# Attention merge moved to VectorE in half rows, a copy moved to ScalarE, and two small TensorE products moved to other PSUM banks

## The chip, the core and the metric

The kernel runs on one core of a Trainium2 chip. The core has five engines that work side by side: TensorE (PE in the profile; its weight loads are listed as PEld), VectorE (DVE), ScalarE (ACT), GpSimd (POOL) and SyncE (SP, which here issues the transfers). The metric is the device time of one execution in microseconds; lower is better. A "bank" is one of the eight parts of the accumulation memory (PSUM) that TensorE writes to and that VectorE and ScalarE read.

## What is computed

One layer of a hybrid decoder for a prompt of 1024 tokens and a sample group of 8 sequences of 8 new tokens (1088 columns in all), float32 throughout. One input projection gives queries, keys and values of three attention groups, gates, and the inputs of a state-space scan. The part that matters here is the merge of the three attention groups, for each pair of heads:

```python
def _combine_groups(outs, lses):
    w = jax.nn.softmax(jnp.stack(lses, 0), axis=0)
    o = jnp.einsum('gblh,gblhd->blhd', w.astype(outs[0].dtype), jnp.stack(outs, 0))
    return o.reshape(o.shape[0], o.shape[1], ATT_WIDTH)
```

that is, att = w0*o0 + w1*o1 + w2*o2, then times SiLU of a gate path. The three groups look back with dilations 1, 4 and 16. Sample attention runs over a cache of past keys and values and is added in the same layout. After that come the scan, two branch projections, an output projection and a final norm.

## The kernel before, in words

Channels lie on the 128 partitions and tokens along the row. The work has four phases: a front (norm and modulation), attention, the scan (SSD) and the output projections. In attention and scan TensorE's main work is the input projection, cut into jobs of 128 output channels (`run`, L260). A job has three chunks of 368, 368 and 352 columns, and each chunk eight steps of three matmuls (`mm3`, L195: high part, low part and cross term), written as "pj" in the profile. Each job loads its weights and splits them into whi (ScalarE, L191) and wlo (VectorE, L192).

**The order on TensorE is the order of the code.** Between the steps of a projection, `Order` lets a generator, the side work, put its own matmuls in. A generator yields a number of nanoseconds (or an event and a number); it goes on when the planned time has passed that. Nothing is waited for on the chip by this: it only places the instructions. The order on the other engines is set by a scheduler when the program is built; it isn't written out in the code. It may run an instruction of later code ahead of one of earlier code.

**Attention.** For each of four head pairs hp and three groups g, `attention` (L548) turns the values (vt, vts; copied out by VectorE, L573 and L576), then `prompt_group` (L590) makes scores (s), which VectorE reduces with the mask (L617) and ScalarE exponentiates (L620), turns the result (pt; copied out by ScalarE L641 and VectorE L639) and multiplies it by the values (o, copied out by ScalarE L661). After group 2 come `sample_scores` and `sample_values` (L766): seven and three small transposes of the sample's probabilities (spt), products with the cached values accumulated in the bank so, a copy of it to the tile so (L798), a pause of the planner (L799), two transposes of the copy (soT, L803) and four VectorE instructions that gate the result into the first group's output (L807). The transposes of the next head pair's values follow soT at once in TensorE's order.

**The merge** is `combine` (L717). Its inputs are the group outputs oT[0..2], in each group's own token order (`group_view`, L477, reads them in natural order: steps of 256 elements for dilation 4 and of 64 for dilation 16), and the weights, which `weights` (L681) wrote to memory and six transfers bring back spread over the partitions (L722, tiles wb). It is traced with `issue_after(last)`: those of its instructions that run on VectorE come after the last L807; its GpSimd instructions aren't held by that. The result goes to memory (L733) and is read in the last phase.

**Banks.** In the attention phase the eight banks are three for projections, two of kind A (scores), two of kind B (transposes) and one of kind C (vts, o, so). In the scan phase they are three, two A and three B. A tile of a kind takes the bank that was taken longest ago and waits until its last reader is done. In the scan phase the side work (L919) turns the tokens of B (to_tokens, kind B, L924), 15,000 planned ns after projection C makes the products CB (kind A, two tiles, masked by VectorE in L938) and one small product for the sample (L940 to L942); after these TensorE goes back to projection steps. Meanwhile VectorE runs the convolution of the next channel tile, three instructions that each use the one before (L869).

Of the kernel before, what the change touches and what calls it, by code (L numbers as in the profile page):

```python
# [11 lines left out]
AF = mybir.ActivationFunctionType  # L12
OP = mybir.AluOpType
# [4 lines left out]
T = 1024  # L18
# [5 lines left out]
DIL = (1, 4, 16)  # L24
# [86 lines left out]
def trunk(ctx: ExitStack, tc: tile.TileContext, I, O):  # L111
    nc = tc.nc
    V, S, G, PE, SP = nc.vector, nc.scalar, nc.gpsimd, nc.tensor, nc.sync
# [15 lines left out]
    def bank(kind):  # L129
        return lambda name: banks[kind].tile([128, 512], F32, tag=kind, name=name)  # L130

    bankA, bankB, bankC, bankPJ = bank("a"), bank("b"), bank("c"), bank("p")
# [15 lines left out]
    def P(name):  # L148
        a, n = PACK[name]
        return pack[:, a:a + n]  # L150
# [11 lines left out]
    def sums(ps, sq, first=True, last=True):  # L162

        for j in range(4):
            PE.matmul(ps[j * 32:j * 32 + 32, :QT], onesc[:, :32], sq[:, j * QT:(j + 1) * QT], start=first, stop=last,
                      tile_position=(0, j * 32))
# [39 lines left out]
    def mm(out, w, x, ns, **kw):  # L206
        PE.matmul(out, w, x, **kw)  # L207
        order.spend(ns)

    def turn(out, x, eye):  # L210
        PE.transpose(out, x, eye)  # L211
        order.spend(110)
# [79 lines left out]
    with pool("ph0", 2) as p0:  # L292
# [51 lines left out]
        with tc.high_priority():  # L344
            ps = bankA("ms")
# [7 lines left out]
            for j in range(4):  # L353
                ps = (bankPJ if j < 3 else bankC)("rb")
# [122 lines left out]
    def group_view(ap, g):  # L477

        return ap.rearrange("p (r i) -> p i r", r=DIL[g])
# [3 lines left out]
    with ExitStack() as actx:  # L483
# [233 lines left out]
        def combine(hp, oT, ga):  # L717
            at = oT[0]
            for g in range(3):
                wb = ap_.tile([128, T], F32, tag="kv", name="wb", bufs=5)  # L720
                for h in range(2):
                    SP.dma_start(out=wb[h * 64:h * 64 + 64], in_=bass.AP(tensor=wt_d.tensor, offset=wt_d[hp, g, h].offset,  # L722
                                                                         ap=[[0, 64], [1, T]]))
                src = group_view(oT[g][:, :T], g)
                if g == 0:
                    V.tensor_mul(at[:, :T], at[:, :T], wb)
                else:
                    d = DIL[g]
                    w3 = wb.rearrange("p (i r) -> p i r", r=d)
                    G.tensor_tensor(w3, src, w3, op=OP.mult)  # L730
                    V.tensor_add(at[:, :T], at[:, :T], wb)
            V.scalar_tensor_tensor(at[:, :T], at[:, :T], 0.5, ga[:, :T], op0=OP.mult, op1=OP.mult)
            SP.dma_start(out=att_d[hp], in_=at)  # L733

        def sample_scores(hp, ks):
# [30 lines left out]
        def sample_values(hp, sm, vs, at):  # L766
            yield 9000.0,
            pT = a1.tile([128, 7, 128], F32, tag="spT", name="spT")
            pN = a1.tile([TS, 3, 128], F32, tag="spN", name="spN")
            for i, n in ((0, 4), (4, 3)):  # L770
                pt = bankB("spt").rearrange("p (x n) -> p x n", n=128)
                for x in range(n):
                    turn(pt[:, x, :], sm[:, (i + x) * 128:(i + x + 1) * 128], ident)
                S.activation(pT[:, i:i + n, :], pt[:, :n, :], AF.Copy)
            pt = bankB("spt").rearrange("p (x n) -> p x n", n=128)
            for g in range(3):
                turn(pt[:TS, g, :], sm[:, 896 + g * TS:896 + (g + 1) * TS], ident)
            S.activation(pN, pt[:TS, :3, :], AF.Copy)

            yield 3000.0,  # L780
            po = bankC("so")
            for g in range(3):
                PE.matmul(po[:, :256].rearrange("p (e n) -> p e n", e=2), pN[:, g, :],
                          vs[:, g:g + 1, :].to_broadcast([TS, 2, 128]), start=g == 0, stop=False)
            vts = []
            for x in range(7):
                vt = ap_.tile([128, NB, 128], F32, tag="kv", name="vt", bufs=5)
                SP.dma_start(out=vt, in_=I["vc"][hp, x])
                vts.append(vt)
            for x, vt in enumerate(vts):  # L790
                if x in (0, 5):
                    yield (500.0 if x == 0 else 8000.0),
                for e in range(2):
                    for j in range(4):
                        mm(po[j * 32:j * 32 + 32, e * 128:(e + 1) * 128], pT[:, x, j * 32:j * 32 + 32],
                           vt[:, 2 * j + e, :], 70.0, start=False, stop=x == 6 and e == 1)
            so = a1.tile([128, 7, 128], F32, tag="spT", name="so")
            V.tensor_copy(so[:, 0:2, :].rearrange("p e n -> p (e n)"), po[:, :256])  # L798
            yield 1500.0,  # L799
            ga = tiles[hp, "ga"]  # L800
            po = bankB("soT")
            for e in range(2):
                turn(po[:, e * 128:(e + 1) * 128], so[:, e, :], ident)  # L803
            for e in range(2):
                for h in range(2):
                    hs = slice(h * 64, h * 64 + 64)
                    last = V.scalar_tensor_tensor(at[hs, T:].rearrange("p (b s) -> p b s", b=NB)[:, e::2, :],  # L807
                                           po[hs, e * 128:(e + 1) * 128].rearrange("p (b x) -> p b x", b=NB)[:, e::2, h * 8:h * 8 + 8],
                                           0.5, ga[hs, T:].rearrange("p (b s) -> p b s", b=NB)[:, e::2, :],
                                           op0=OP.mult, op1=OP.mult)  # L810
            return last
# [9 lines left out]
    with ExitStack() as bctx:  # L821
# [3 lines left out]
        cb = b1.tile([128, 24], F32, name="cb")  # L825
# [93 lines left out]
        def side():  # L919
            for gr in range(4):  # L920
                yield ("B", gr), 15000.0
                B = BT, BS = tiles.pop(("B", gr))
                Bk = b1.tile([128, 9, 128], F32, tag="Bk", name="Bk")
                to_tokens(B, lambda c0, n, ps: S.activation(Bk[:, c0:c0 + n, :], ps, AF.Copy))  # L924

                Bs = b1.tile([128, 128], F32R, tag="Bs", name="Bs")
                S.activation(Bs, Bk[:, 8, :], AF.Copy)
                V.tensor_sub(Bs[TS:], Bk[TS:, 8, :], Bs[TS:].bitcast(F32))
                yield ("C", gr), 15000.0
                CT, CS = tiles.pop(("C", gr))  # L930
                CB = b1.tile([128, TT], F32, tag="CB", name="CB")
                G.memset(CB[TS:, T:], 0.0)
                for q in range(2):
                    ps = bankA("cb").rearrange("p (c n) -> p c n", c=4)
                    for c in range(4):
                        sl = slice((4 * q + c) * 128, (4 * q + c + 1) * 128)
                        mm(ps[:, c, :], BT[:, sl], CT[:, sl], 224.0, start=True, stop=True)
                    V.tensor_tensor(CB[:, q * 512:(q + 1) * 512].rearrange("p (c n) -> p c n", c=4), ps,  # L938
                                    P("causal")[:, None, :].to_broadcast([128, 4, 128]), op=OP.mult)
                ps = bankA("cb")  # L940
                mm(ps[:TS, :TS], BS[:, :TS], CS[:, :TS], 224.0, start=True, stop=True)
                V.tensor_tensor(CB[:TS, T:], ps[:TS, :TS], P("causal_s")[:TS], op=OP.mult)  # L942
                order.passed.add(("B", gr))
                sq = b1.tile([128, TT], F32, tag="sq", name="sq")
                for xt in range(4 * gr, 4 * gr + 4):
                    yield from x_tile(gr, xt, Bk, Bs, CB, CT, CS, sq)
                    order.passed.add(("x", xt))

                yield 4000.0,
                ps = bankB("ms")  # L950
                sums(ps, sq)
                ms = bp.tile([128, 3, QT], F32, tag="ms", name="ms", bufs=1)
                rms(ms, ps, 512)
                for j in range(4):
                    SP.dma_start(out=rs_d[gr:gr + 1, j * QT:(j + 1) * QT], in_=ms[j * 32:j * 32 + 1, 1, :])
# [147 lines left out]
    with pool("yr", 2) as yr, pool("yw", 2) as yw:  # L1103
# [31 lines left out]
        for gr in range(5):  # L1135
            if gr:
                if gr < 4:
                    ys = load_ys(gr)
                else:
                    ys = []  # L1140
                    for i in range(4):
                        x = yr.tile([128, TT], F32, tag="yx", name="ax")
                        SP.dma_start(out=x, in_=att_d[i])
                        ys.append(split(x))
            for m in range(8):
# [14 lines left out]
                for c0, cn in CHUNKS:  # L1160
                    sl = slice(c0, c0 + cn)
                    ps = bankPJ("pj")
# [23 lines left out]
    for t in range(9):  # L1186
        n = min(128, TT - t * 128)
        x = f2.tile([128, D], F32, tag="fx", name="fx")
# [6 lines left out]
        for i in range(m):  # L1195
            ps = bankA("fo")[:n, :w]
            cs = slice(i * w, (i + 1) * w)
# [14 lines left out]
        for i in range(2):  # L1212
            cs = slice(i * 512, (i + 1) * 512)
# [152 lines left out]
```

## Time and profile before

| what | us |
|---|---|
| median of 3 runs (1919.27 to 1925.73) | 1921.6 |
| the profiled execution, its own time | 1926.49 |
| its span, first to last instruction | 1924.7 |
| TensorE busy | 1872.7 (97%) |
| VectorE busy | 1020.1 (53%) |
| ScalarE busy | 664.1 (35%) |
| GpSimd busy | 393.2 (20%) |
| mean granted clock of TensorE | 0.992 |

The span is one execution; an engine's busy time is the part of it in which it had an instruction running. A timeline row gives the start, the length, the engine, the line of the code, the operation, output and inputs with partitions x elements, and in brackets how long the engine had been idle before and what ended that idle time. "x2" means that adjacent instructions were merged into one row. The granted clock is a share of TensorE's full 2.4 GHz.

### The profile page before, as it was taken

The page shows a single profiled execution, that of the slowest core. Times are in us where ns is not written, and L with a number is a line of the kernel's source. Part 1 is how long each engine was busy: PE and PEld are TensorE (multiplying, and loading weights), DVE is VectorE, ACT ScalarE, POOL GpSimd, SP SyncE. Part 2 cuts the span into 40 slices and gives each one's busy share as a digit, 9 for nine tenths or more (in the row PEclk, how much of TensorE's full clock was granted, in tenths as well). Part 3 has the DMA queues.
Part 4 walks back from the last instruction along what each step waited for, and adds up shares of the span by engine and source line. Part 5 has one row for each costly group of instructions (what it writes and reads, how often), then busy time and mean ns, then how long its engine had stood idle before and what let it go on. Part 6 is the DMA issues. An engine that isn't in the chain of part 4 may idle for free.

```text
span 1924.7 us, 32199 instructions
## 1 busy us (share of the span) xinstructions
PE 1872.7 (97%) x13057; PEld 1748.8 (91%) x13057; DVE 1020.1 (53%) x1918; ACT 664.1 (35%) x1271; POOL 393.2 (20%) x584
## 2 busy tenths in 40 slices
PE   6999999999999999999999999999999999999998
PEld 4999989989998998999989998999898989999987
DVE  4633243334334323467675776577657665566654
ACT  4434234314432432424352434243433332131222
POOL 3100010010001001124513542444244300000400
PEclk8999999999999999999999999999999999999999
DMA  8422562273246227435444444444233364364322
GB/s 329 138 79 92 158 200 83 90 220 114 96 159 194 84 89 240 143 121 171 148 142 137 148 154 132 137 138 138 82 102 105 126 223 137 121 196 153 119 88 77
DMA packets 108949, 269.56 MB, mean 140 GB/s; under 512 B 41581, under 2 KB 50593, under 8 KB 105537
## 3 DMA queue, kind: packets, MB, share of 16 engines
q1 hardware_dynamic: 108800, 267.51, 42.2%
q8 instruction: 102, 1.67, 0.4%
q14 instruction: 47, 0.38, 0.1%
HBM read 224.93 MB, written 80.26 MB: 159 GB/s over the span
## 4 chain that ended last, share of the span: by engine, by line
PE 58%; DVE 4%; ACT 3%; DMA 2%; issue 1%; POOL 0%; DVEq 0%; ACTq 0%; POOLq 0%
PE pj L198 15%; PE pj L199 15%; PE pj L200 15%; PE fo L1203 2%; PE fo L1201 2%; PE fo L1202 2%; PE yd L207 2%; PE yo L207 2%; DMA csb<-cs_d 2%; PE stt L207 1%; PE tt L211 1%; DVE xc L869 1%; PE sts L207 1%; DMA yx<-u_d 1%; PE o L207 0%
## 5 line engine op out<-in xcount | busy, mean ns | idle before, releaser
L198 PE MATMUL pj<-h_hi,whi 128*128 128x368 f32 x2256 | 753.9, 334 | 0.0
L199 PE MATMUL pj<-h_hi,wlo 128*128 128x368 f32 x2256 | 739.1, 328 | 0.0
L200 PE MATMUL pj<-h_lo,whi 128*128 128x368 f32 x2256 | 739.0, 328 | 0.0
L198 PEld LDWEIGHTS pj<-h_hi,whi 128*128 128x128 f32 x2256 | 424.8, 188 | 25.3 <-issue 22.8
L199 PEld LDWEIGHTS pj<-h_hi,wlo 128*128 128x128 f32 x2256 | 425.0, 188 | 0.7
L200 PEld LDWEIGHTS pj<-h_lo,whi 128*128 128x128 f32 x2256 | 424.6, 188 | 0.0
L192 DVE TENSOR_TENSOR wlo<-wraw,whi 128x1024 fp32r<-128x1024 f32 (+1 forms) x136 | 158.1, 1162 | 253.6 <-ACT whi L191 251.7
L191 ACT ACTIVATE whi<-wraw 128x1024 fp32r<-128x1024 f32 (+1 forms) x136 | 126.5, 930 | 351.6 <-PE pj L200 334.3
L198 PE MATMUL pj<-yhi,whi 128*128 128x368 f32 (+1 forms) x480 | 158.3, 330 | 2.5 <-DVE acc L1165 2.5
L199 PE MATMUL pj<-yhi,wlo 128*128 128x368 f32 (+1 forms) x480 | 157.8, 329 | 0.1
L200 PE MATMUL pj<-ylo,whi 128*128 128x368 f32 (+1 forms) x480 | 157.5, 328 | 0.0
L620 ACT ACTIVATE pr<-pr,st 128x128 f32<-128x128 f32 (+1 forms) x192 | 83.9, 438 | 89.3 <-DVE st L617 89.2
L198 PEld LDWEIGHTS pj<-yhi,whi 128*128 128x128 f32 x480 | 90.6, 189 | 5.4 <-DVE acc L1165 3.0
L199 PEld LDWEIGHTS pj<-yhi,wlo 128*128 128x128 f32 x480 | 90.7, 189 | 1.8 <-DVE wlo L192 0.4
L200 PEld LDWEIGHTS pj<-ylo,whi 128*128 128x128 f32 x480 | 90.5, 189 | 0.0
L869 DVE SCALAR_TENSOR_TENSOR xc<-raw,cw,xc 128x1112 f32<-128x1112 f32 x60 | 82.5, 1376 | 10.6 <-ACT xc L867 9.8
L639 DVE COPY pT<-pt 128x512 f32<-128x512 f32 x40 | 27.6, 689 | 102.3 <-ACT pT L641 40.4
L1170 POOL TENSOR_TENSOR acc<-acc,ta 128x368 f32<-128x368 f32 (+1 forms) x24 | 24.2, 1010 | 253.1 <-DVE ta L1169 253.1
L559 POOL COPY ks<-k 128x64 f32<-128x64 f32 x12 | 6.7, 558 | 301.5 <-DVE k L500 301.5
L997 POOL TENSOR_TENSOR xde<-xdt,tok 128x256 f32<-128x256 f32 x64 | 43.1, 702 | 120.3 <-DVE xdt L990 120.3
L500 DVE COPY k<-pj 128x368 f32<-128x368 f32 (+2 forms) x44 | 24.1, 581 | 81.3 <-PE pj L200 79.8
L964 DVE TENSOR_TENSOR csb<-tok,csb 128x2048 f32<-128x2048 f32 x16 | 39.4, 2464 | 46.8 <-DMA csb<-cs_d 43.1
(269 smaller groups left out, 2613.5 us busy)
## 6 DMA issues: line engine op xcount, KB each, us to landing
wraw<-in_w_in SPq DMA_DIRECT2D x96, 512.0 KB
csb<-cs_d SPq DMA_DIRECT2D x16, 1088.0 KB
kt<-in_kc SPq DMA_DIRECT2D x32, 448.0 KB
out_kc<-in_kc SPq DMA_DIRECT2D x32, 448.0 KB
out_vc<-in_vc SPq DMA_DIRECT2D x28, 512.0 KB
vt<-in_vc SPq DMA_DIRECT2D x28, 512.0 KB
sg_d<-sg SPq DMA_DIRECT2D x16, 544.0 KB
ecs<-cs_d SPq DMA_DIRECT2D x32, 272.0 KB
```

Of the source, the lines that this page charges most:

```text
L191: S.activation(hi, raw, AF.Copy)
L192: V.tensor_sub(lo, raw, hi.bitcast(F32))
L198: PE.matmul(ps, whi[:, k, :], xhi[k], start=first and k == 0, stop=False)
L199: PE.matmul(ps, wlo[:, k, :], xhi[k], start=False, stop=False)
L200: PE.matmul(ps, whi[:, k, :], xlo[k], start=False, stop=last and k == n - 1)
L207: PE.matmul(out, w, x, **kw)
L620: S.activation(pr[:, h, c0:c0 + m], pr[:, h, c0:c0 + m], AF.Exp, scale=-1.0, bias=st[:, 0, h, u:u + 1], accum_out=st[:, 1, h, u:u + 1])
L869: V.scalar_tensor_tensor(c, raw[:, t:t + CONV], cw[:, j, t:t + 1], c, op0=OP.mult, op1=OP.add)
L964: V.tensor_tensor(csb[:, :, :T].rearrange("p h (c l) -> p h c l", l=CH), tok[:, :8, 32 + h0:34 + h0].rearrange("p c h -> p h c")[:, :, :, ...
L997: G.tensor_tensor(xde[:, c:c + 2].rearrange("p c (h d) -> p c h d", h=2), xdt[:, c:c + 2, :].rearrange("p c (h d) -> p c h d", h=2), tok[: ...
L1201: PE.matmul(ps, hi, whi[:, k, cs], start=k == 0, stop=False)
L1202: PE.matmul(ps, lo, whi[:, k, cs], start=False, stop=False)
```

## The change

In the merge, the two multiplications by weights that GpSimd did for each head pair go to VectorE, and all the merge's arithmetic is cut into two halves of 512 columns. The copy of the sample outputs goes from VectorE to ScalarE, and the planner's pause before soT goes from 1500 to 2500 ns. The third batch of sample transposes takes a bank of kind C in place of B; the scan's small product takes one of kind B in place of A.

```diff
@@ combine, from L724 @@
                 src = group_view(oT[g][:, :T], g)
-                if g == 0:
-                    V.tensor_mul(at[:, :T], at[:, :T], wb)
-                else:
-                    d = DIL[g]
-                    w3 = wb.rearrange("p (i r) -> p i r", r=d)
-                    G.tensor_tensor(w3, src, w3, op=OP.mult)
-                    V.tensor_add(at[:, :T], at[:, :T], wb)
-            V.scalar_tensor_tensor(at[:, :T], at[:, :T], 0.5, ga[:, :T], op0=OP.mult, op1=OP.mult)
+                d = DIL[g]
+                w3 = wb.rearrange("p (i r) -> p i r", r=d)
+                for x in range(2):
+                    cs = slice(x * 512, x * 512 + 512)
+                    i = slice(x * 512 // d, (x + 1) * 512 // d)
+                    if g == 0:
+                        V.tensor_mul(at[:, cs], at[:, cs], wb[:, cs])
+                    else:
+                        V.tensor_tensor(w3[:, i], src[:, i], w3[:, i], op=OP.mult)
+                        V.tensor_add(at[:, cs], at[:, cs], wb[:, cs])
+                    if g == 2:
+                        V.scalar_tensor_tensor(at[:, cs], at[:, cs], 0.5, ga[:, cs], op0=OP.mult, op1=OP.mult)
             SP.dma_start(out=att_d[hp], in_=at)
@@ sample_values, L775 @@
-            pt = bankB("spt").rearrange("p (x n) -> p x n", n=128)
+            pt = bankC("spt").rearrange("p (x n) -> p x n", n=128)
@@ sample_values, L798 @@
-            V.tensor_copy(so[:, 0:2, :].rearrange("p e n -> p (e n)"), po[:, :256])
-            yield 1500.0,
+            S.activation(so[:, 0:2, :].rearrange("p e n -> p (e n)"), po[:, :256], AF.Copy)
+            yield 2500.0,
@@ side, L940 @@
-                ps = bankA("cb")
+                ps = bankB("cb")
                 mm(ps[:TS, :TS], BS[:, :TS], CS[:, :TS], 224.0, start=True, stop=True)
```

## Rows read from the trace of the kernel before

**Rows 1.** The page, part 1: busy time, share of the span and instructions of each engine

```profile
PE 1872.7 (97%) x13057; PEld 1748.8 (91%) x13057; DVE 1020.1 (53%) x1918; ACT 664.1 (35%) x1271; POOL 393.2 (20%) x584
```

**Rows 2.** Waits of PE: engine, line, releaser: us in total, times, longest

```profile
PE soT L211 <- DVE so L798: 6.0, 3, 2.5
PE cb L207 <- DVE CB L938: 4.7, 4, 1.7
PE yo L207 <- DVE sta L1023: 3.5, 3, 1.2
PE spt L211 <- ACT spT L774: 3.2, 4, 0.8
PE pt L211 <- ACT pr L620: 0.8, 1, 0.8
```

**Rows 3.** Timeline of PE, first merge: start us, us, instruction [idle before <-releaser]

```profile
263.87 0.44 PE L211 MATMUL soT<-pack,so 128*128 128x128 f32 x2 [1.81 <-DVE so L798]
265.28 0.63 PE L211 MATMUL vt<-pack,vT 128*128 128x128 f32 x4 [0.54 <-DVE oT L807]
272.46 0.82 PE L211 MATMUL pt<-pack,pr 128*128 128x128 f32 x6
```

**Rows 4.** Timeline of DVE, first merge

```profile
260.02 3.46 DVE L192 TENSOR_TENSOR wlo<-wraw,whi 128x1024 fp32r<-128x1024 f32 x1 [0.40 <-ACT whi L191]
263.40 0.41 DVE L798 COPY so<-so 128x256 f32<-128x256 f32 x1
264.34 0.80 DVE L807 SCALAR_TENSOR_TENSOR oT<-soT,ga 64x32 f32<-64x32 f32 x4 [0.53 <-PE soT L211]
265.17 2.12 DVE L726 TENSOR_TENSOR oT<-oT,wb 128x1024 f32<-128x1024 f32 x1
267.31 1.29 DVE L573 COPY v<-vt 128x512 f32<-128x512 f32 x2
268.71 1.21 DVE L731 TENSOR_TENSOR oT<-oT,wb 128x1024 f32<-128x1024 f32 x1
269.85 0.27 DVE L617 CUSTOM_DVE_ANT_0 pr<-s,msk 128x128 f32<-128x128 f32 x1
```

**Rows 5.** Timeline of POOL, first merge

```profile
259.48 6.72 POOL L730 TENSOR_TENSOR wb<-oT,wb 128x1024 f32<-128x1024 f32 x2 [27.60 <-DMA wb<-wt_d]
```

**Rows 6.** Timeline of DVE and PE, third merge

```profile
594.08 1.23 DVE L192 TENSOR_TENSOR wlo<-wraw,whi 128x1024 fp32r<-128x1024 f32 x1 [0.40 <-ACT whi L191]
596.37 0.80 DVE L807 SCALAR_TENSOR_TENSOR oT<-soT,ga 64x32 f32<-64x32 f32 x4 [0.73 <-PE soT L211]
603.18 0.28 DVE L617 CUSTOM_DVE_ANT_0 pr<-s,msk 128x128 f32<-128x128 f32 x1
605.52 0.93 PE L211 MATMUL pt<-pack,pr 128*128 128x128 f32 x5 [0.77 <-ACT pr L620]
```

**Rows 7.** Windows, behind the fourth merge: us, busy of PE, PEld, DVE, ACT, POOL, PEclk, DMA

```profile
765.00:769.50 4.50, 4.41 (x18) 4.41 (x19) 3.81 (x7) 0.43 (x1) 2.45 (x1) 0.62 0.63 233
```

**Rows 8.** Timeline of ACT, first merge

```profile
270.17 0.40 ACT L620 ACTIVATE pr<-pr,st 128x128 f32<-128x128 f32 x1 [10.18 <-DVE st L617]
272.88 0.38 ACT L641 ACTIVATE pT<-pt 128x256 f32<-128x256 f32 x1 [0.25 <-PE pt L211]
```

**Rows 9.** Timeline of DVE: key copies of a group with dilation 1, then 4

```profile
207.60 0.54 DVE L500 COPY k<-pj 128x368 f32<-128x368 f32 x1 [0.83 <-PE pj L200]
248.58 0.84 DVE L500 COPY k<-pj 128x368 f32<-128x368 f32 x1 [5.52 <-PE pj L200]
```

**Rows 10.** Timeline of DVE in the SSD phase, first small product

```profile
816.52 1.38 DVE L869 SCALAR_TENSOR_TENSOR xc<-raw,cw,xc 128x1112 f32<-128x1112 f32 x1 [0.63 <-ACT xc L867]
817.93 1.29 DVE L938 TENSOR_TENSOR CB<-cb,pack 128x512 f32<-128x512 f32 x2
819.14 1.37 DVE L869 SCALAR_TENSOR_TENSOR xc<-raw,cw,xc 128x1112 f32<-128x1112 f32 x1
820.42 0.21 DVE L942 TENSOR_TENSOR CB<-cb,pack 64x64 f32<-64x64 f32 x1
```

## The prediction

> **What bounds the kernel now.** I read the page's busy shares first: TensorE works 1872.7 us of a span of 1924.7 us, VectorE 53% of it, ScalarE 35%, GpSimd 20% [rows 1]. No other engine is near the span, so the time can fall only by the 52 us in which TensorE does nothing, or by a higher clock. The second view is the list of TensorE's waits [rows 2], and here the reader should look for the products that the diff touches. Three are there: the turn of the sample outputs (soT) waits 6.0 us behind their copy on VectorE, the small product of the scan phase (cb) 4.7 us behind the evacuation of the bank that it takes over, and the third sample transpose (spt) 3.2 us in the same way. Together that is 13.9 us.
>
> The third view is the timeline of one merge, engine by engine, to see why the copy is late. TensorE stands 1.81 us before soT [rows 3]. The copy L798 needs 0.41 us, but it starts at 263.40, behind a wlo subtraction of 3.46 us [rows 4]. That subtraction runs beside the two multiplications of GpSimd, 259.48 to 266.20 [rows 5]. Before the third merge the same subtraction starts ahead of GpSimd's and takes 1.23 us [rows 6]; there soT doesn't wait, which is why rows 2 count three waits for four merges. So GpSimd's work delays VectorE by some 2.2 us, and TensorE pays.
>
> The wait has a tail. Behind the fourth, the longest with 2.5 us, the granted clock is 0.62 over 4.5 us [rows 7], a mix of the two levels, 1.2 and 2.4 GHz: (1 - 0.62) x 4.5 = 1.7 us more.
>
> **The change part by part.**
> *Small product from bank kind A to B.* In the scan phase A has two buffers and both hold the two products just made; B has three, last used by the turns of B's tokens, which the planner puts 15 us earlier. The four waits go: -4.7. Behind the product TensorE has projection steps, which need nothing from VectorE, so nothing takes their place at once.
>
> *Third transpose from B to C.* C's one buffer is free since the last attention output was copied. The four waits go: -3.2. The next user of C, the accumulation of the sample outputs, now stands behind the copy of this transpose, but it reads that copy's result anyway, and the planner puts 3.0 us between.
>
> *Copy of the sample outputs on ScalarE, and 1.0 us more before soT.* ScalarE copied 128x256 from a bank in 0.38 us and had been idle for 10.18 us until 270.17 in the first merge [rows 8]. The cover is that idle stretch; without it TensorE would wait for what stands ahead of the copy on ScalarE, less the extra 1.0 us. The extra 1.0 us is two projection steps put ahead of soT instead of behind it, no added work. The three waits go: -6.0, and with them the slow clock: -1.7.
>
> *Merge on VectorE.* Gone are eight GpSimd multiplications and what they cost VectorE. A merge had four whole-row VectorE instructions; the second kind, L731, takes 1.21 us undisturbed, while L726 took 2.12 beside GpSimd [rows 4]. It will have twelve half-row ones. A 128x512 piece takes 1.29 / 2 = 0.65 us in a row as the two v copies did [rows 4]. That holds for the eight pieces that read and write in order. The other four read the group's output in steps of 256 or 64 elements, and the trace has no such read. Lower bound: 0.65, as if the step were free. Upper bound: GpSimd's own pace for it, 6.72 / 4 = 1.68 us a half. The nearest row is VectorE's own write in the same steps, 0.84 us against 0.54 for 368 in order [rows 9]; 0.65 x 0.84 / 0.54 = 1.0 us, and I take that. A rule of the Trainium skill speaks against the change here: SBUF — State Buffer, section Door 1, says that accesses that keep crossing into a new 16-byte line pay a penalty, which such a read always does. It gives no price; by it the 1.0 stands, and if only writes paid, the price would be 0.65 and my sum 4.2 us better. The merge is then 8 x 0.65 + 4 x 1.0 = 9.2 us of VectorE.
>
> That length costs nothing by itself; what matters is what queues behind it. After soT, TensorE turns the next group's values and makes its scores; VectorE must copy those (L573) and reduce the scores (L617), ScalarE the exponentials, before TensorE comes to pt. In the third merge L617 began 603.18 - 597.17 = 6.0 us after L807 ended and pt waited 0.77 [rows 6]; in the first it was 4.7 [rows 4] and pt didn't wait [rows 3]. So pt waits for whatever goes beyond 5.2 us. Which instructions of the merge go ahead of L617? The order is fixed when the program is built. In the scan phase a chain of three L869, each needing the one before, takes turns with products that became ready meanwhile, though their code stands later [rows 10]. So I expect the same here: the six pieces that need no other piece (two halves of group 0's product, four of the others') go first, 2 x 0.65 + 4 x 1.0 = 5.3 us, then the copies of v, 1.3, then L617 among the additions: 6.6 us or so, a wait of 1.4 at each of the first three merges, 4.2 in all, in place of the 0.8 of today. The bounds: 0 if the copies and L617 go first; if the whole merge goes ahead, 9.2 + 1.3 - 5.2 = 5.3 each. The fourth merge has no attention behind it, so its delay is covered by projections.
>
> *Sum.* -4.7 - 3.2 - 6.0 - 1.7 - 0.8 + 4.2 = -12.2 us. The profiled execution took 1926.5 us, 4.9 above the median of the runs; I take those 4.9 as common to both kernels. It would become 1914.3, the median 1921.6 - 12.2 = 1909.4.
>
> **The rivals.**
> *The merge as one block.* All twelve pieces run before the v copies and L617. For it: they stand earlier in the code and all are ready at once, as their weights have landed. Against it: rows 10. Price: 3 x 5.3 = 15.9 of waits at pt, each longer than the 2.5 us behind which the clock fell, so 3 x 1.7 = 5.1 more: 16.4 gained, 21.0 lost, 1926.2. With the reads at GpSimd's pace the merge is 8 x 0.65 + 4 x 1.68 = 11.9, each wait 8.0, the loss 24.0 + 5.1 = 29.1: 1934.3, slower. It decides from a loss of 22.2 us on.
> *The gains come back.* TensorE arrives earlier but the vector chains don't: cb's 4.7 returns at yo, which waits three times for the state chain already (3.5 us, [rows 2]), and soT's 6.0 as waits at pt or vt (vt waits 0.54 for L807 today, [rows 3]). What is left is 3.2 + 1.7: 1916.7. Against it: those chains start from TensorE's own products and so move with it.
> *The change does less than it says,* because the copy lands behind a late instruction on ScalarE: rows 8 leave little room for that. soT's 6.0 and the 1.7 would stay and the sum be -4.5: 1917.1. I give it 0.03, counted with the case before.
>
> **How the numbers follow.** A measurement of this kernel can tell about 0.3%, 5.8 us, from no change. The likeliest case, 0.60, runs from no wait at pt (-16.4: 1905.2) to waits of 2.4 each (-9.2: 1912.4): all of it faster. The block, 0.23: half of it the dearer reads or more, 0.12 slower and 0.11 within. The gains that come back, or a late copy, 0.17: mostly within, 0.14, and 0.03 faster. That makes 0.63 faster, 0.25 the same, 0.12 slower. The range goes from 1904 to 1926, which leaves out the slower block and the tail below.
>
> **What would show it.** Right: no row of PE waits for soT or for cb behind L938, and none for spt; the granted clock behind the fourth merge is 1.00; wlo subtractions near the merge take 1.2 us; the half pieces with steps take about 1.0 us and those without 0.65; L617 starts 6 to 7 us after L807 and pt waits 1 to 2 us in three places. Wrong: a row of pt waits of 10 us or more with twelve pieces in one stretch on VectorE, pieces of 1.6 us, or new waits at yo and cb that make up for those gone.

## The result and the profile after

The changed kernel takes 1912.37 us (median of 7 runs, 1906.95 to 1917.44) against 1922.19 us (7 runs) of the kernel before on the same chip: a ratio of 0.9943, with an interval of 0.9927 to 0.9958. The forecast was 1909.4 against 1921.6, a ratio of 0.9937, which lies inside. The profiled execution took 1912.37 us, with a span of 1910.6; the mean granted clock is 0.992 as before. Ratios are over fast runs; the one slow run of all is one of 4428.77 us among the six of the kernel with whole rows (e5 below), whose median of 1909.21 us counts it. Lines behind the merge stand five lower in the file than before (L807 is L812, L938 is L943).

Page, part 1 of the changed kernel (busy time, share of the span, instructions), answering to [rows 1]:

```profile
PE 1871.7 (98%) x13057; PEld 1747.7 (91%) x13057; DVE 1023.6 (54%) x1946; ACT 665.1 (35%) x1275; POOL 359.7 (19%) x576
```

GpSimd loses 33.5 us and VectorE gains only 3.5, although it took over all eight multiplications: it is no longer held up beside GpSimd, and its four copies of 0.4 us are gone. TensorE's busy time falls by 1.0 us of the 14.1 by which the span falls, so nearly all of the gain has to be in its waits. The list of them, answering to [rows 2]:

```profile
PE yo L207 <- DVE sta L1028: 3.1, 3, 1.2
PE pt L211 <- ACT pr L620: 2.7, 3, 1.0
PE cb L207 <- DVE CT L881: 2.5, 1, 2.5
...
PE ms L165 <- POOL sq L1098: 2.1, 1, 2.1
PE vt L211 <- DVE oT L812: 1.6, 3, 0.5
PE pj L198 <- DVE acc L1170: 0.7, 1, 0.7
```

The reader is to see what is absent: no row for soT, none for spt, none for cb behind L943. The three waits that the diff aimed at, 13.9 us, are gone. pt has risen from 0.8 to 2.7, and ms behind sq is new.

VectorE's timeline in the first merge, answering to [rows 4]:

```profile
259.52 1.23 DVE L192 TENSOR_TENSOR wlo<-wraw,whi 128x1024 fp32r<-128x1024 f32 x1 [0.40 <-ACT whi L191]
262.81 0.80 DVE L812 SCALAR_TENSOR_TENSOR oT<-soT,ga 64x32 f32<-64x32 f32 x4 [2.06 <-PE soT L211]
263.63 1.29 DVE L732 TENSOR_TENSOR oT<-oT,wb 128x512 f32<-128x512 f32 x2
264.84 4.07 DVE L734 TENSOR_TENSOR wb<-oT,wb 128x512 f32<-128x512 f32 x4
268.94 1.29 DVE L573 COPY v<-vt 128x512 f32<-128x512 f32 x2
...
270.35 0.27 DVE L617 CUSTOM_DVE_ANT_0 pr<-s,msk 128x128 f32<-128x128 f32 x1
...
270.90 0.68 DVE L735 TENSOR_TENSOR oT<-oT,wb 128x512 f32<-128x512 f32 x1
...
272.06 1.88 DVE L735 TENSOR_TENSOR oT<-oT,wb 128x512 f32<-128x512 f32 x3
```

wlo takes 1.23 us in place of 3.46. Then come the six pieces that need no other piece, the copies of v, and the first reduction L617, with the additions L735 behind and among the reductions. That is the order that the forecast drew from [rows 10]. A piece with steps takes 4.07 / 4 = 1.02 us, one without 0.65. L617 starts 270.35 - 263.61 = 6.74 us after L812 ends.

The copy on ScalarE, in that engine's timeline, starts as soon as the accumulation ends:

```profile
259.98 0.39 ACT L803 ACTIVATE so<-so 128x256 f32<-128x256 f32 x1 [0.49 <-PE so L207]
```

TensorE's timeline of the changed kernel, with the first merge, the one wait of the scan for CT, and the first or last rows of some phases (s are the scores that follow pt):

```profile
70.92 0.33 PE L198 MATMUL pj<-h_hi,whi 128*128 128x368 f32 x1
...
262.39 0.38 PE L211 MATMUL soT<-pack,so 128*128 128x128 f32 x2
...
271.39 0.27 PE L211 MATMUL pt<-pack,pr 128*128 128x128 f32 x1
272.37 0.93 PE L211 MATMUL pt<-pack,pr 128*128 128x128 f32 x5 [0.71 <-ACT pr L620]
273.23 1.13 PE L207 MATMUL s<-k,q 64*128 64x256 f32 x8
...
798.03 0.27 PE L211 MATMUL tt<-pack,xcs 128*128 128x128 f32 x1
...
995.54 3.57 PE L207 MATMUL cb<-CT,xc 128*128 128x128 f32 x16 [2.48 <-DVE CT L881]
...
1530.24 2.15 PE L165 MATMUL ms<-sq,onesc 128*32 128x272 f32 x8
...
1801.60 0.40 PE L1206 MATMUL fo<-wohi,yhi 128*128 128x512 f32 x1
```

The kernel before, at the same places except for cb, where the longer of its two waits for CT is shown, one group of the scan later (pt of the first merge is in [rows 3]):

```profile
70.41 0.33 PE L198 MATMUL pj<-h_hi,whi 128*128 128x368 f32 x1
...
273.21 1.14 PE L207 MATMUL s<-k,q 64*128 64x256 f32 x8
...
804.90 0.27 PE L211 MATMUL tt<-pack,xcs 128*128 128x128 f32 x1
...
1190.32 2.05 PE L207 MATMUL cb<-CT,xc 128*128 128x128 f32 x16 [2.40 <-DVE CT L876]
...
1540.51 2.15 PE L165 MATMUL ms<-sq,onesc 128*32 128x272 f32 x8
...
1578.28 0.67 PE L198 MATMUL pj<-yhi,whi 128*128 128x368 f32 x1 [2.48 <-DVE acc L1165]
...
1815.71 0.40 PE L1201 MATMUL fo<-wohi,yhi 128*128 128x512 f32 x1
```

These rows divide the 14.1 us between the two spans (1924.7 - 1910.6). At the first small transposes of the scan (tt) the changed kernel is 6.9 us ahead, 7.4 counted from the first projection steps; that is attention. At the last sums of the scan (ms) it is 10.3 ahead: the scan gave 3.4. At the first steps of fo it is 14.1 ahead: 3.8 more in the output phase, which the change doesn't touch. There TensorE waited 2.48 us for acc in the profiled execution of before and 0.7 in that of after, and behind the longer wait the granted clock is 0.89 over the 15 us from 1575, while it is 1.00 over the 15 us from 1565 in the changed kernel.

Only the first part of this division is steady. A second profiled execution of the changed kernel (f1 below) has the same instructions in the same order on every engine, and its gain divides into 6.9 us for attention, 5.4 for the scan and 1.5 for the output phase, against 7.4, 3.4 and 3.8 here. Whether the change has a part in the wait for acc is open: the five traces with both banks, the merge on VectorE behind the gating and the scan's products where they were (after, e5, e6, f1, f2) have 0.7 to 1.1 us there, the other nine 1.9 to 2.5. The 14.1 us between the two profiled executions are more than the 10.9 that the runs give (0.0057 x 1922.2); that of before took 1926.49 us, 4.3 above its median.

### The profile page after: what moved, and what is told of

Read it like the earlier page. It is cut to its first block, busy times and chain, and to the rows that moved or that the text cites. A ratio compares the mean times of both kernels' runs of the same rounds, so it can differ in the third digit from the quotient of the medians.

```text
span 1910.6 us, 32219 instructions
## 1 busy us (share of the span) xinstructions
PE 1871.7 (98%) x13057; PEld 1747.7 (91%) x13057; DVE 1023.6 (54%) x1946; ACT 665.1 (35%) x1275; POOL 359.7 (19%) x576
## 4 chain that ended last, share of the span: by engine, by line
PE 87%; DVE 5%; DMA 4%; ACT 2%; issue 1%; POOL 1%; SPq 0%; ACTq 0%; POOLq 0%; DVEq 0%
PE pj L198 22%; PE pj L199 21%; PE pj L200 21%; PE o L207 2%; PE pt L211 2%; PE s L207 2%; PE fo L1208 2%; PE fo L1206 2%; PE fo L1207 2%; PE yo L207 2%; DMA csb<-cs_d 2%; PE yd L207 2%; PE early L242 1%; PE stt L207 1%; PE tt L211 1%
## 5 line engine op out<-in xcount | busy, mean ns | idle before, releaser
L192 DVE TENSOR_TENSOR wlo<-wraw,whi 128x1024 fp32r<-128x1024 f32 (+1 forms) x136 | 151.0, 1110 | 204.9 <-ACT whi L191 203.0
L1175 POOL TENSOR_TENSOR acc<-acc,ta 128x368 f32<-128x368 f32 (+1 forms) x24 | 24.2, 1009 | 249.2 <-DVE ta L1174 249.2
```

Of the source, the lines that this page charges most:

```text
L192: V.tensor_sub(lo, raw, hi.bitcast(F32))
```

## The experiments

Twelve kernels, timed in five rounds each (the one with reads in order in three). Ratios are against the kernel before, run beside them.

### One part of the change at a time

The first four kernels are the kernel before with one part of the diff each.

```diff
@@ e1_scan_bank @@
-                ps = bankA("cb")
+                ps = bankB("cb")
@@ e2_transpose_bank @@
-            pt = bankB("spt").rearrange("p (x n) -> p x n", n=128)
+            pt = bankC("spt").rearrange("p (x n) -> p x n", n=128)
@@ e3_copy @@
-            V.tensor_copy(so[:, 0:2, :].rearrange("p e n -> p (e n)"), po[:, :256])
-            yield 1500.0,
+            S.activation(so[:, 0:2, :].rearrange("p e n -> p (e n)"), po[:, :256], AF.Copy)
+            yield 2500.0,
@@ e4_merge: the hunk of combine as it stands in the change @@
```

**The scan's bank alone.** Expected:

> The kernel before with the scan's small product alone in a bank of kind B. My theory: the four waits of cb behind the masking of CB (4.7 us) go and nothing takes their place: 1922 - 4.7 = 1917.5, ratio 0.9976, and the waits of yo behind the state chain stay at 3.5. Rival (TensorE only arrives earlier at the next vector chain): the waits at yo and at the next cb grow by as much, and the ratio is 1.000.

Measured: 1916.75 us, ratio 0.9966 (0.9953 to 0.9979), 6.5 us. Its waits of TensorE no longer list cb behind CB, cb waits 0.6 us for CT (3.7 before), and soT is

```profile
PE soT L211 <- DVE so L798: 3.9, 2, 2.1
```

The 4.7 us went and did not come back at yo (3.0, 3.5 before) or cb. New is a wait of 2.1 us for ms behind sq, which other kernels below have without this edit. soT also fell, by 2.1, though nothing near it was edited.

**The transpose's bank alone.** Expected:

> The kernel before with the third sample transposes alone in the bank of kind C. My theory: the four waits of spt (0.8 each, 3.2 us) go: ratio 0.9983, the waits at soT stay at about 6.0. Rival (gain comes back): the accumulation of the sample outputs, next in bank C, or soT waits 3 us more in all, ratio 1.000.

Measured: 1918.41 us, ratio 0.9971 (0.9957 to 0.9986), 5.6 us. spt has gone, 3.2 us; other waits, most of them far from the edit, moved with it (cb behind CB 3.0 us, pt 2.0):

```profile
PE ms L165 <- POOL sq L1093: 4.2, 2, 2.1
...
PE soT L211 <- DVE so L798: 2.4, 1, 2.4
```

What follows from both: a bank edit removes its own wait in full, and other waits of 1 to 4 us come and go with it. A new order on the other engines, as the scheduler builds it, is not needed for that: in this second kernel VectorE and GpSimd run their instructions in the order of the kernel before, and soT waits once in place of three times. Its wait hangs on a race. GpSimd starts when the weights' transfer has landed ([rows 5]); in the kernel before it starts 0.1 to 0.7 us ahead of wlo in the three merges where soT waits, and 1.3 us behind it in the third. Here it starts ahead of wlo in the fourth merge alone. Shifts of a microsecond settle that.

**The copy and the pause alone.** Expected:

> The kernel before with the copy of the sample outputs on ScalarE and the pause of 2500 ns; GpSimd still multiplies. Theory one (the copy only stood in the wrong queue): the three waits at soT (6.0) and the slow clock behind the fourth merge (1.7) go, though the wlo subtraction beside GpSimd still takes 3.3 us or more; ratio 0.996. Theory two (GpSimd's slowing of VectorE is what costs): the wait moves from soT to vt, because the gating behind soT stands behind the same slow subtraction: vt's waits grow from 1.6 by 1 us a merge or more, and the ratio is above 0.998.

Measured: 1915.28 us, ratio 0.9952 (0.9937 to 0.9968), 9.2 us. There is no wait of soT. VectorE's timeline in the first merge shows that wlo is still held up:

```profile
261.23 3.27 DVE L192 TENSOR_TENSOR wlo<-wraw,whi 128x1024 fp32r<-128x1024 f32 x1 [0.41 <-ACT whi L191]
```

So the copy doesn't need a quick wlo once it is off VectorE. It ends 2.0 us ahead of soT in this merge as in that of the changed kernel (259.98 + 0.39 against 262.39), so the 1.0 us more of pause was not needed for it. The pause alone was not run.

**The merge alone.** Expected:

> The kernel before with the merge alone on VectorE in halves; the copy stays on VectorE, pause 1500 ns. Theory two (GpSimd's slowing is what costs): the subtraction takes 1.23 us, the copy is done before soT's turn, the waits at soT go without ScalarE (-6.0 and -1.7), pt waits 2.7 us as in the whole change against 0.8: ratio 0.997. Theory one (the queue is what costs): soT still waits 3 us or more in all. If both theories hold, either edit alone ends the waits at soT, and the parts add up to more than the whole change.

Measured: 1920.27 us, ratio 0.9985 (0.9975 to 0.9996), 2.9 us. VectorE's timeline in the first merge:

```profile
261.30 1.23 DVE L192 TENSOR_TENSOR wlo<-wraw,whi 128x1024 fp32r<-128x1024 f32 x1 [0.40 <-ACT whi L191]
```

With GpSimd out of the way wlo takes 1.23 us, the copy on VectorE is in time, and soT waits nowhere. The pt waits are 2.5 us (three times), as with the whole change. So **either of the two edits ends the soT waits**; the sum counted these once, which was right, but their gain belongs to neither edit alone. The four parts come to 6.5 + 5.6 + 9.2 + 2.9 = 24.2 us one by one and to 10.9 together: they share the soT waits, which fell by 2.1, 3.6, 6.0 and 6.0 us, 17.7 in all where the whole change can end 6.0. The rest of the difference is not divided.

### What the form of the merge costs

**Whole rows in place of halves**, all else as in the change:

```diff
-                for x in range(2):
-                    cs = slice(x * 512, x * 512 + 512)
...
+                if g == 0:
+                    V.tensor_mul(at[:, :T], at[:, :T], wb)
+                else:
+                    V.tensor_tensor(w3, src, w3, op=OP.mult)
+                    V.tensor_add(at[:, :T], at[:, :T], wb)
```

> The kernel after with the merge in whole rows of 1024 in place of halves. My theory (what counts is the work ahead of L617, 5.3 us in pieces, and whole rows hold the same): the first multiplication 1.2 us and the two stepped ones 2.0 each, then the copies of v; L617 begins 6.5 to 7 us after the gating as in the kernel after (6.74), then whole additions of 1.2 us come between the reductions: pt waits 1 to 1.5 us a merge against 0.7 to 1.0, the time within 3 us of the kernel after, ratio 0.994 to 0.996. Rival (the halves let the reductions in early): pt waits 3 us a merge or more, ratio over 0.998.

Measured: 1909.21 us, ratio 0.9922 (0.9902 to 0.9942). VectorE's timeline, with the last reduction before the additions, and then the wait of TensorE:

```profile
265.60 3.92 DVE L730 TENSOR_TENSOR wb<-oT,wb 128x1024 f32<-128x1024 f32 x2
...
270.95 0.27 DVE L617 CUSTOM_DVE_ANT_0 pr<-s,msk 128x128 f32<-128x128 f32 x1
...
271.71 0.41 DVE L617 CUSTOM_DVE_ANT_0 pr<-s,msk 128x256 f32<-128x256 f32 x1
...
272.06 2.47 DVE L731 TENSOR_TENSOR oT<-oT,wb 128x1024 f32<-128x1024 f32 x2
```

```profile
PE pt L211 <- ACT pr L620: 0.7, 3, 0.2
```

Halves are not needed for the short wait. L617 starts 6.5 us after the gating ends (at 264.42), hardly earlier than with halves, yet pt waits 0.7 in all in place of 2.7. With halves a ready addition slips in between the second reduction and the third (0.68 us at 270.90 in the timeline after); whole rows leave all four reductions ahead of the additions, which start at 272.06. pt's second turn needs the exponential of the third reduction: counted from the end of the gating that one ends at 8.61 us with halves and 8.13 with whole rows, 0.48 earlier, as much as the first merge's wait falls (0.71 to 0.23). The order among reductions and additions thus does as much as the length of the merge.

**Reads in order.** The multiplication reads a group's output as it lies, so that groups 1 and 2 enter the merge in their own token order:

```diff
-                        V.tensor_tensor(w3[:, i], src[:, i], w3[:, i], op=OP.mult)
+                        V.tensor_tensor(wb[:, cs], oT[g][:, cs], wb[:, cs], op=OP.mult)
```

> The kernel after with the four multiplications reading the group's output in the order in which it lies, without the steps of 256 and 64 elements (so groups 1 and 2 are merged in the wrong token order). My theory (the step of the read is what makes the piece 1.02 us): the pieces take 0.65 us, 1.5 us less work a merge, L617 begins 5.2 us after the gating and pt waits 0.2 us in all or not at all: 2.5 us under the kernel after. Rival (a piece that writes onto its own second input costs 1.02 whatever the step): pieces stay at 1.02 and pt at 2.7.

Measured: 1906.7 us, ratio 0.991 (0.9887 to 0.9933).

```profile
262.42 0.79 DVE L812 SCALAR_TENSOR_TENSOR oT<-soT,ga 64x32 f32<-64x32 f32 x4 [2.06 <-PE soT L211]
...
264.46 2.49 DVE L734 TENSOR_TENSOR wb<-oT,wb 128x512 f32<-128x512 f32 x4
...
268.38 0.27 DVE L617 CUSTOM_DVE_ANT_0 pr<-s,msk 128x128 f32<-128x128 f32 x1
```

The same piece takes 2.49 / 4 = 0.62 us in order and 1.02 with steps, so the steps cost 0.40 us a piece. L617 then starts 5.17 us after the gating, and no row of TensorE waits at pt. With 5.17 us the forecast's threshold of 5.2 is met from below, and as forecast nothing waits. The Trainium skill (SBUF — State Buffer, section Door 1) says that accesses which keep crossing into a new 16-byte line pay a penalty; this pair of kernels agrees, for steps in one of the two inputs; wb, which is the other input and the output, lies in order in both kernels.

**Multiplications ahead of the pause.** The transfers of the weights and the four multiplications are traced before the pause, with the additions left behind soT:

```diff
+            wbs = weigh(hp, oT)
-            yield 2500.0,
+            yield 2500.0,
...
-                    combine(hp, oT, tiles.pop((hp, "ga")))
+                    combine(hp, oT, tiles.pop((hp, "ga")), wbs)
```

> The kernel after with the transfers of the weights and the four stepped multiplications of a merge written ahead of the pause before soT, so that they need not come behind the gating; VectorE is idle there for 2.06 us or more. My theory (pt waits for what stands ahead of L617): only the rest stands between the gating and L617, which begins 3 to 5 us after the gating; pt waits 0 in place of 2.7, and if a multiplication runs over into the gating, vt waits up to 1 us a merge more: between 2.7 less and 0.3 more than the kernel after, ratio 0.9925 to 0.9945. Rival (pt's wait comes from ScalarE's queue, where the evacuation of q stands among the exponentials): pt keeps 2 us or more.

Measured: 1925.28 us, ratio 1.0007 (0.9989 to 1.0025). The expectation failed. pt's wait did go, but a larger one took its place, in VectorE's timeline and TensorE's waits:

```profile
263.33 3.89 DVE L732 TENSOR_TENSOR wb<-oT,wb 128x512 f32<-128x512 f32 x4 [6.51 <-DMA wb<-wt_d]
...
267.73 1.21 DVE L192 TENSOR_TENSOR wlo<-wraw,whi 128x1024 fp32r<-128x1024 f32 x1
268.86 0.78 DVE L822 SCALAR_TENSOR_TENSOR oT<-soT,ga 64x32 f32<-64x32 f32 x4
```

```profile
PE vt L211 <- DVE oT L822: 12.9, 3, 5.2
```

Here VectorE kept to its order: it stood 6.51 us until the weights' transfer had landed, with wlo and the gating behind, and TensorE's vt turns wait for the gating. The clock fell behind the wait as well: 0.57 granted over the 8 us from 268. Placing the merge behind the gating also keeps VectorE from reaching wb before the transfer has landed.

### Which parts of the change are needed

**Without the merge:** both banks, the copy and the pause, with the merge as in the kernel before.

```diff
 (the change without its hunk of combine)
```

> The kernel before with both banks and the copy on ScalarE with its pause, GpSimd still multiplying. My theory (the copy off VectorE already ends the waits at soT, the merge on VectorE only lengthens what stands ahead of L617): no wait at soT, spt or cb behind CB, pt 1 us in all or none: as fast as the kernel after or up to 3 us faster, ratio 0.992 to 0.9945. Rival (the merge is what gives the whole change its gain): waits at soT, vt or pt of 4 us or more in all, and the ratio is 0.996 or above.

Measured: 1908.01 us, ratio 0.9917 (0.9893 to 0.9941). soT, spt, cb behind CB and pt wait nowhere. VectorE still stands beside GpSimd, in their timelines:

```profile
259.06 3.80 DVE L192 TENSOR_TENSOR wlo<-wraw,whi 128x1024 fp32r<-128x1024 f32 x1 [0.41 <-ACT whi L191]
...
263.60 3.05 DVE L726 TENSOR_TENSOR oT<-oT,wb 128x1024 f32<-128x1024 f32 x1
```

```profile
258.85 6.72 POOL L730 TENSOR_TENSOR wb<-oT,wb 128x1024 f32<-128x1024 f32 x2 [26.93 <-DMA wb<-wt_d]
```

Little on TensorE waits for that stretch: in this merge vt waits 0.95 us in place of 0.54, as the gating stands behind wlo. So moving the merge buys hardly anything that shows once the copy is on ScalarE, and it adds the waits at pt. That the kernel without it is faster isn't shown, since the intervals overlap.

**Without the copy:** banks and merge as in the change, the copy and the pause of 1500 ns as before. It ran beside the changed kernel again and two more.

```diff
-            S.activation(so[:, 0:2, :].rearrange("p e n -> p (e n)"), po[:, :256], AF.Copy)
-            yield 2500.0,
+            V.tensor_copy(so[:, 0:2, :].rearrange("p e n -> p (e n)"), po[:, :256])
+            yield 1500.0,
```

> The changed kernel again, beside the next three on one chip, so that they can be set against it directly. Both theories expect the ratio of the first measurement, 0.994, within its interval 0.993 to 0.996.

> The changed kernel with the copy of the sample outputs back on VectorE and the pause of 1500 ns back; merge and both banks stay. Theory one, either edit alone is enough for soT: GpSimd multiplies nothing, the wlo subtraction ahead of the copy takes 1.2 us, so the copy is in time, soT waits under 1 us in all, the pt waits stay near 2.7, and the time is within 2 us of the changed kernel (ratio 0.993 to 0.996). Theory two, the copy on ScalarE and the longer pause are needed in the changed kernel: soT waits 3 us or more, with slow clock behind it, and the time is 4 to 8 us above the changed kernel (ratio 0.996 to 0.999).

Measured: the changed kernel again 1913.39 us, 0.9941 (0.9925 to 0.9956); without the copy 1909.22 us, 0.992 (0.990 to 0.994). In VectorE's timeline of the latter wlo takes 1.22 us, the copy follows at once, and soT waits nowhere; pt waits 2.5:

```profile
257.54 1.22 DVE L192 TENSOR_TENSOR wlo<-wraw,whi 128x1024 fp32r<-128x1024 f32 x1 [0.40 <-ACT whi L191]
```

Theory one holds as to the mechanism: either edit is enough, shown now by leaving out the one and the other. As to the time, both theories expected no gain over the changed kernel, and 1909.22 lies 4 us under it; the intervals overlap, so that it is faster isn't shown.

**The scan's products later.** The wait of 2.48 us for CT, with the slow clock behind it, is the largest wait left in the scan. Two kernels ask for the products 2.5 us later: the changed kernel, and that with whole rows.

```diff
-                yield ("C", gr), 15000.0
+                yield ("C", gr), 17500.0
```

> The changed kernel with 17500 planned ns instead of 15000 ahead of the scan's products CB. Theory one, the wait of 2.5 us for CT in the second group and the slow clock behind it (16 products in 3.57 instead of 2.05 us) are an accident of when the products are asked for: both go, about 4 us less than the changed kernel (ratio 0.992), while yo stays near 3. Theory two, the wait moves: yo or ms grows by as much, the time stays (0.994).

> The changed kernel with the merge in whole rows on VectorE and 17500 planned ns ahead of the scan's products. Theory one: pt waits 0.7 as with whole rows before, the wait of 1.4 for CT goes with its slow clock; 2 us less than whole rows alone, ratio 0.990 to 0.992. Theory two, the wait moves to yo or ms: as whole rows alone, 0.992.

Measured: 1912.24 us, 0.9933 (0.9910 to 0.9955), and with whole rows 1907.6 us, 0.9912 (0.9892 to 0.9932). cb behind CT has gone in both. In the first, the list of TensorE's waits now has 2.4 us for acc and 1.5 us for pj behind raw. Neither stands where either theory looked (yo is 3.0 us, ms behind sq has gone). The changed kernel gained 1 us where 4 were expected, which can't be told from none: nearer to theory two. Whole rows with the later scan is the lowest median beside the changed kernel on its chip, 1907.6 against 1913.4, but its interval overlaps that of whole rows alone; that the delay adds anything isn't shown. The changed kernel itself, run again, waits 1.5 us for CT and not 2.48.

## Why the prediction was right, step by step

**What bounds the kernel.** Right: the gain came out of TensorE's waits and the slow clock behind some of them. By the list they fell in attention, from the first projection steps to tt, from 11.6 us (6.0 + 3.2 + 1.6 + 0.8) to 4.7 (2.7 + 1.6 + 0.4), 6.9 of the 7.4 us found there.

**The two banks, -4.7 and -3.2.** Right; e1 and e2 show each wait gone by itself, and no wait of the same size behind. In the scan 3.4 of the 4.7 are seen. The rest was given back elsewhere in this trace: 2.1 us for ms behind sq, which the list of before does not have, and one CT wait with the clock fallen behind it, against two CT waits before (3.7 us) with the clock up. That clock is in the window view of the changed kernel (us, busy of five engines, PEclk, DMA share, GB/s):

```profile
995.00:1000.00 5.00, 4.46 (x22) 4.28 (x23) 4.49 (x7) 1.77 (x4) 1.96 (x5) 0.66 0.28 39
760.50:765.00 4.50, 4.50 (x29) 4.47 (x28) 3.77 (x8) 0.48 (x1) 0.00 (x0) 1.00 0.49 200
```

After the stand of 2.48 us the granted clock is 0.66 over 5 us, a mix of 1.2 and 2.4 GHz, and the sixteen products take 3.57 us where the kernel before, at 1190.32 after a stand of 2.40, took 2.05 at a clock of 1.00. A wait of that length does not always bring the slow level. In the second trace of the changed kernel, with a CT wait of 1.5 us, the scan gave 5.4.

**The copy, -6.0, and the clock, -1.7.** The waits went, and behind the fourth merge the clock is 1.00 in place of 0.62 (second row; [rows 7]). The two windows bear out the 1.7: in 4.5 us TensorE ran 29 matmuls in place of 18, and at 4.5 / 29 = 0.16 us each the 11 more are worth about 1.7 us. That 7.4 us found less 6.9 of listed waits leaves only 0.5 does not speak against it, since a wait costs more than its listed idle time (see the merge). The step that was wrong without harm is the reason: not only this edit ends the waits, the merge does it as well (e4, f2).

**The merge, +4.2 in place of 0.8.** The order was right in every piece: six pieces, copies of v, L617. 1.02 us a piece with steps against 1.0 taken, 0.65 without against 0.65, 6.74 us to L617 against 6.6. By the list the wait was put too high: 2.7 us in all (0.71 to 1.0 each) where 1.4 each was forecast. But the list counts idle time alone. From the first turn of pt to the scores behind it TensorE takes 273.21 - 272.46 = 0.75 us in the first merge of before, where nothing waits, and 273.23 - 271.39 = 1.84 us in that of after: 1.09 lost with 0.71 listed. The second and third merges lose 1.38 and 1.36 by the same rows (the third of before 1.15). That is 3.8 us against the 4.2 forecast. "pt waits for whatever goes beyond 5.2 us" gives 6.74 - 5.2 = 1.5 for the 1.09 of the first merge. e5 shows what the step left out: what pt waits for is the third reduction, and its place among the additions counts as well as the start of the first.

**The sum.** -12.2 forecast, -10.9 measured (-14.0 to -8.1 by the interval). As far as these rows separate them, each term was found within some 2 us; that the sum comes nearer is in part luck, as the scan's share was 3.4 us in one trace and 5.4 in another. That the 4.9 us between the profiled execution and the median are common to both kernels was wrong: the profiled execution after stands on its median.

**The rivals.** The merge as one block did not come: [rows 10] was the better guide than the order of the code. The gains didn't come back at yo (3.1 against 3.5) or vt (1.6 as before), and the copy is in time.

## What to carry to other kernels

When two edits both end the same wait, each looks like a gain alone and one of them is idle, or dear, in the pair: try the change without each part (here the pair of banks with either edit had lower medians, 1908.0 and 1909.2, than the whole, though the intervals overlap). An engine that works in order should get the independent pieces of a long job before the chain that others wait for only if these pieces are short and their inputs are there; one instruction waiting for a transfer stops all behind it. Waits of a few us that hang on a race, as wlo against a transfer, come and go with edits elsewhere, and some differ by 1 us between two executions of one program, so the gains of parts need not add up. The idle time that a list of waits gives is less than what the wait costs.

## What was not expected of the hardware

A VectorE instruction with two inputs that comes second beside a GpSimd multiplication seems to wait until that one is done. GpSimd's two multiplications are one row in most traces; with the scan's bank alone they are listed apart:

```profile
258.52 2.91 POOL L730 TENSOR_TENSOR wb<-oT,wb 128x1024 f32<-128x1024 f32 x1 [27.56 <-DMA wb<-wt_d]
261.59 3.65 POOL L730 TENSOR_TENSOR wb<-oT,wb 128x1024 f32<-128x1024 f32 x1 [0.16 <-issue]
```

There wlo (3.41 us from 259.11) ends at 262.52, 1.09 us after the first of the two. If the first takes 2.91 us elsewhere too, it ends at 262.39 in the kernel before and at 261.76 without the merge, and wlo at 263.48 and 262.86, 1.09 and 1.10 later; the second ends at 266.20 and 265.57, and L726 at 267.29 and 266.65, 1.09 and 1.08 later. So wlo's 3.46 and 3.80 us are what is left of GpSimd's when it starts, and 1.1 us more, nearly the whole of an undisturbed one (1.21 to 1.23). GpSimd pays too. In the second merge of the kernel without the merge edit, where wlo is nearly done when GpSimd starts and nothing of VectorE's runs between, its two take 5.77 us, not 6.72; in the first merge with the transpose's bank alone VectorE's wlo comes first, keeps its 1.23 us, and GpSimd's two take 7.58:

```profile
424.90 5.77 POOL L730 TENSOR_TENSOR wb<-oT,wb 128x1024 f32<-128x1024 f32 x2 [27.71 <-DMA wb<-wt_d]
```

```profile
258.21 1.23 DVE L192 TENSOR_TENSOR wlo<-wraw,whi 128x1024 fp32r<-128x1024 f32 x1 [0.40 <-ACT whi L191]
```

```profile
258.49 7.58 POOL L730 TENSOR_TENSOR wb<-oT,wb 128x1024 f32<-128x1024 f32 x2 [27.40 <-DMA wb<-wt_d]
```

The Trainium skill (SBUF — State Buffer, section Who interferes with whom) says that such an instruction contends with a GpSimd instruction that reads the same memory, and that the order of issue decides which of the two waits. The rows agree, in both orders: the one that came second waited.
